# Giving the last split quarter of each gate and up tile its own buffers, and filling them one step later

## The chip, the cores and the metric

The kernel runs on one core of a Trainium2 chip. A core has a matrix engine (PE in the profile, with its weight loads shown apart as PEld), a vector engine (DVE), a scalar engine (ACT), a third elementwise engine (POOL) and a queue (SP) that issues most of the transfers from main memory. All of them run side by side and wait for each other through semaphores. The metric is the time of one execution in microseconds; less is better.

## The reference

One step of a decoder trunk over 520 tokens (512 new ones and 8 single continuations), width 1024, all in 32-bit floats: a half-step feed-forward block, a mixer, a second half-step feed-forward block and a last normalization. The change touches only the two feed-forward blocks:

```
def _swiglu(x, wg, wu, wd):
    return (jax.nn.silu(x @ wg) * (x @ wu)) @ wd
h = h + 0.5 * _swiglu(_rms_norm(h, ffn1_norm), ffn1_w_gate, ffn1_w_up, ffn1_w_down)
...
h = h + 0.5 * _swiglu(_rms_norm(h, ffn2_norm), ffn2_w_gate, ffn2_w_up, ffn2_w_down)
```

The gate and up matrices are 1024 by 2816, the down matrix 2816 by 1024. The 2816 columns are 22 tiles of 128, counted f = 0 to 21.

## The kernel before, in words

**Numbers in two parts.** A 32-bit product is computed as three faster ones. A weight tile is split into a rounded part (`whi`, a cast on ACT, L106) and the remainder (`wlo`, a subtraction on DVE, L107); `mm3` (L116 to L118) then issues high by high, high by low and low by high. Such a pair of buffers comes from the function `split`, whose buffers are 1024 columns wide and belong to a named ring: `whi`/`wlo` with three buffers each, `shi`/`slo` with two each.

**A step.** For each f from 2 (first block) or 1 (second block) on, the tokens are taken in two halves and gate and up together in seven products instead of eight, a scheme that multiplies sums of weight tiles with sums of token tiles. `load(f)` fetches the raw gate and up tiles (two transfers of 512 KB, L250 and L251, into one of two buffers of the ring `raw`), splits the gate tile (`d1`, traced as whi_fa), forms sums of quarters (`s1` at L257, `s2` at L258 and L259), splits these (`e1`, `e2`, traced as shi_fc and shi_fd) and splits the last quarter of the up tile, 512 columns (`d2`, traced as whi_fb). `product(f, p)` is one of the seven: twelve matmuls (four pieces of depth times three). Product 4 is the only one that uses `d2`. ACT copies intermediate sums out of the accumulators (`ac`, L285), `gates` and `close` make the activated tile `g` (L291 to L301).

**The order in which `step` asks for them.** product(f, 1), which calls `load(f)`; then product(f-1, 4) and close(f-1); then the products 5, 6, 3, 7, 2 of f. So product 4 of a tile comes one step after its other six.

**Chunks.** After tiles 0 to 7, 8 to 15 and 16 to 21 of g, the down product runs over what is there: eight output tiles d, each with a weight unit of up to 1024 columns that `load_unit` loads into half of a `raw` buffer and splits into the ring `whi`/`wlo` (48 matmuls a unit in the first two chunks; traced as whi_1d and whi_2d, dn). Before it, product(hi+1, 1), product(hi, 4) and close(hi) are asked for, so that at this edge one tile of the next chunk is loaded already. In the last chunk of the second block (`down_by_half`) units 0 and 1 are split into `whi`/`wlo`, 2 and 3 into `shi`/`slo`, and 4 to 7 into buffers of their own that become free when product(21, 4) is done.

**What sets the order on an engine.** The program is written down once in the order above; then a planner with a modelled timeline lays out, for each engine and for the transfer queue, the instructions that can run, earlier-written ones first, so that products of the next tile may fill a time in which an earlier-written matmul isn't ready. On the chip every engine follows its list strictly: an instruction that waits holds up all behind it. A buffer of a ring is given to its next user when the last reader of its previous content is done, and a transfer waits in the queue until its buffer is free.

**In the second block** sixteen small state updates go along with the steps: two transfers in on SP (`br`, `hs`, L796 and L798), eight scalings on ACT (L813), and an adding and a storing transfer from POOL (L814, L815).

The change's lines are `split`, the end of `load`, and the head of `product`.

Of the kernel before, what the change touches and what calls it, by code (L numbers as in the profile page):

```python
# [10 lines left out]
F32R = mybir.dt.float32r  # L11
# [5 lines left out]
P = 128  # L17
# [44 lines left out]
def tile_trunk_step(ctx: ExitStack, tc: tile.TileContext, ins: dict, outs: dict):  # L62
# [7 lines left out]
    wp = ctx.enter_context(tc.tile_pool(name="wp", bufs=3, side="right"))  # L70
# [19 lines left out]
    def raw_pair(name):  # L90
        return wp.tile([P, 2, 1024], F32, tag="raw", bufs=2, name=f"raw_{name}")
# [6 lines left out]
            half.extend([t[:, 1], t[:, 0]])  # L98
        return half.pop()

    def split(src, n, name, hp, nb, tags):
        hi, lo = (hp.tile([P, 1024], F32R, tag=t, bufs=nb, name=f"{t}_{name}")[:, :n] for t in tags)
        h, l = hi, lo
        if len(src.shape) == 3:
            h, l = (t.rearrange("p (j c) -> p j c", j=src.shape[1]) for t in (hi, lo))
        nc.scalar.copy(h, src)  # L106
        nc.vector.tensor_tensor(out=l, in0=src, in1=h.bitcast(F32), op=ALU.subtract)  # L107
        return hi, lo

    def load_unit(src, n, name):  # L110
        raw = raw_tile(name)[:, :n]
        nc.sync.dma_start(out=raw, in_=src)
        return split(raw, n, name, wp, 3, ("whi", "wlo"))

    def mm3(ps, whi, wlo, xhi, xlo, start, stop, **kw):
        nc.tensor.matmul(ps, whi, xhi, start=start, stop=False, **kw)  # L116
        nc.tensor.matmul(ps, whi, xlo, start=False, stop=False, **kw)  # L117
        nc.tensor.matmul(ps, wlo, xhi, start=False, stop=stop, **kw)  # L118

    def ws(w, k, m=P):  # L120
        return w[:, k * m : (k + 1) * m]
# [73 lines left out]
    class Ffn:  # L195
# [50 lines left out]
        def load(self, f):  # L246
            i, wx, src = self.i, self.wx, ins[f"w{self.i}gu"]
            n = f"{i}_{f}"
            raw = raw_pair(n)
            nc.sync.dma_start(out=raw[:, 0], in_=src[2 * f])  # L250
            nc.sync.dma_start(out=raw[:, 1], in_=src[2 * f + 1])  # L251
            d1 = split(raw[:, 0], 1024, f"{n}a", wp, 3, ("whi", "wlo"))
            s1 = wx.tile([P, 2, 512], F32, tag="sw", bufs=2, name=f"s1_{n}")
            s2 = wx.tile([P, 2, 512], F32, tag="sw", bufs=2, name=f"s2_{n}")
            up0 = raw[:, 1, :512].unsqueeze(1).to_broadcast([P, 2, 512])
            diag = bass.AP(up0.tensor, up0.offset - 1024, [up0.ap[0], (1536, 2), up0.ap[2]])
            nc.vector.tensor_tensor(out=s1, in0=diag, in1=up0, op=ALU.add)  # L257
            nc.vector.tensor_tensor(out=s2[:, 0], in0=s1[:, 1], in1=raw[:, 0, :512], op=ALU.add)  # L258
            nc.vector.tensor_tensor(out=s2[:, 1], in0=s2[:, 0], in1=raw[:, 0, 512:], op=ALU.add)  # L259
            e1 = split(s1.rearrange("p q c -> p (q c)"), 1024, f"{n}c", wx, 2, ("shi", "slo"))  # L260
            e2 = split(s2.rearrange("p q c -> p (q c)"), 1024, f"{n}d", wx, 2, ("shi", "slo"))
            d2 = split(raw[:, 1, 512:], 512, f"{n}b", wp, 3, ("whi", "wlo"))
            self.w[f] = {1: (d1, 0), 2: (d1, 4), 7: (e1, 0), 5: (e1, 4), 6: (e2, 0), 3: (e2, 4), 4: (d2, 0)}

        def product(self, f, p):
            js = range(KD // 2)
            if f not in self.A:
                with tc.issue_after(self.behind[f]) if f in self.behind else nullcontext():
                    self.load(f)
                n = f"{self.i}_{f}"  # L270
                self.A[f] = ps[0].tile([P, 512], F32, tag="A", bufs=2, name=f"A{n}")
                self.BE[f] = ps[0].tile([P, 2, 512], F32, tag="BE", bufs=2, name=f"BE{n}")
                self.ac[f] = [self.wx.tile([P, 2, HB], F32, tag="ac", bufs=3, name=f"ac{n}_{q}") for q in range(2)]
            slot, dst, opens = {1: (0, 0, True), 2: (1, 1, True), 5: (3, 2, True), 6: (5, 0, False),
                                3: (2, 2, False), 7: (4, 0, False), 4: (6, 0, False)}[p]
            out = self.A[f] if dst == 0 else self.BE[f][:, dst - 1]
            (whi, wlo), k0 = self.w[f][p]
            xth, xtl = self.nx[:2]
            for j in js:
                mm3(out[:, :HB], ws(whi, k0 + j), ws(wlo, k0 + j), xth[:, j, slot], xtl[:, j, slot], opens and j == 0,  # L280
                    j == KD // 2 - 1, skip_group_check=True)
            a, c = self.ac[f]
            keep = {1: a[:, 0], 6: a[:, 1], 7: c[:, 0], 5: c[:, 1]}.get(p)
            if keep is not None:
                nc.scalar.copy(keep, out[:, :HB])  # L285
            if p == 7:
                nc.vector.tensor_tensor(out=c[:, 0], in0=c[:, 0], in1=c[:, 1], op=ALU.add)
# [797 lines left out]
```

## Time and profile before

| what | value |
|---|---|
| runs, median (lowest to highest) | 1020.13 us (1017.38 to 1020.46), 3 runs |
| profiled execution, its own time | 1019.81 us |
| profiled execution, span | 1018.0 us |
| granted PE clock over the span | 0.992 |
| first block, steps and downs | about 26 to 360 us of the span |
| mixer | about 350 to 640 us |
| second block | about 640 to 1000 us |

The profile has a page with the busy share of each engine, and views that answer for a stretch of time or for a tile: the instructions in order of time (start, duration, engine, line, operation, names, shape, count, and in brackets the idle time before it with what ended it), the waits summed over the span (total, times, longest), and the busy time of each engine in given windows (duration of the window, then busy time and count for PE, PEld, DVE, ACT and POOL, the granted clock, the share of the transfer engines and GB/s).

### The profile page before, as it was taken

Reading aid. Unit: us, or ns where it says so; the run is one execution under the profiler, and the core shown is the slowest. Engines: PE = TensorE matmul, PEld = TensorE weight load, DVE = VectorE, ACT = ScalarE, POOL = GpSimd, SP = SyncE. Lnnn points to the kernel's source line nnn. Section 1 sums busy time; section 2 is a strip of 40 time slices with the busy share of each in tenths; the row PEclk is TensorE's granted clock in tenths of the full one; section 3 lists DMA queues with packets and bytes.
Section 4 is the critical chain, followed back from the end, with each engine's and each line's share of the span. In section 5 each row is a group of like instructions: output and inputs, shape, how many; then the busy total and the mean of one; then the engine's idle time right before and its main releaser. Section 6 shows DMA issues by size and latency. Waiting matters only on the chain.

```text
span 1018.0 us, 19402 instructions
## 1 busy us (share of the span) xinstructions
PE 979.7 (96%) x7850; PEld 955.5 (94%) x7850; DVE 790.3 (78%) x1344; ACT 539.9 (53%) x941; POOL 82.8 (8%) x141
## 2 busy tenths in 40 slices
PE   7999999999999999999999989999999999999994
PEld 6999999999999999999899989899999999999993
DVE  7899556995569688688989987999745898447865
ACT  7566323664146455685854235668623787226542
POOL 0000000000000000157211000001100111001000
PEclk9999999999999999999999999999999999999997
DMA  5333222332223232353244321335623556334303
GB/s 175 125 124 120 89 83 87 122 98 101 93 83 104 86 109 106 113 188 116 90 144 149 116 83 53 124 111 163 189 97 115 159 181 187 126 97 135 104 32 84
DMA packets 49193, 118.65 MB, mean 117 GB/s; under 512 B 6664, under 2 KB 17864, under 8 KB 49104
## 3 DMA queue, kind: packets, MB, share of 16 engines
q1 hardware_dynamic: 45520, 109.03, 32.5%
q0 software_dynamic: 3584, 8.39, 3.5%
q8 instruction: 61, 1.00, 0.4%
q14 instruction: 28, 0.23, 0.1%
HBM read 105.86 MB, written 7.34 MB: 111 GB/s over the span
## 4 chain that ended last, share of the span: by engine, by line
PE 85%; DVE 5%; ACT 5%; issue 2%; DMA 2%; POOL 0%; SPq 0%; DVEq 0%; ACTq 0%
PE dn L116 7%; PE dn L118 7%; PE dn L117 7%; PE A L116 7%; PE A L117 6%; PE A L118 6%; PE BE L116 5%; PE BE L118 5%; PE BE L117 5%; PE P L229 4%; PE wo L116 2%; PE wo L118 2%; PE wo L117 2%; PE inz L116 2%; PE inz L118 2%
## 5 line engine op out<-in xcount | busy, mean ns | idle before, releaser
L357 DVE SCALAR_TENSOR_TENSOR td<-dn,r_f 128x520 f32<-128x520 f32 x40 | 27.8, 698 | 112.8 <-PE dn L118 112.8
L116 PE MATMUL dn<-g,whi_1d 128*128 128x260 f32 x352 | 99.5, 283 | 1.8 <-ACT whi_1d L106 1.6
L117 PE MATMUL dn<-g,whi_1d 128*128 128x260 f32 x352 | 99.5, 283 | 0.0
L118 PE MATMUL dn<-g,wlo_1d 128*128 128x260 f32 x352 | 99.1, 282 | 0.0
L116 PE MATMUL dn<-g,whi_2d 128*128 128x260 f32 x256 | 72.5, 283 | 1.6 <-ACT whi_2d L106 1.6
L117 PE MATMUL dn<-g,whi_2d 128*128 128x260 f32 x256 | 72.3, 282 | 0.0
L118 PE MATMUL dn<-g,wlo_2d 128*128 128x260 f32 x256 | 72.2, 283 | 0.0
L116 PEld LDWEIGHTS dn<-g,whi_1d 128*128 128x128 f32 x352 | 66.2, 188 | 2.4 <-ACT whi_1d L106 2.0
L117 PEld LDWEIGHTS dn<-g,whi_1d 128*128 128x128 f32 x352 | 66.3, 188 | 0.0
L118 PEld LDWEIGHTS dn<-g,wlo_1d 128*128 128x128 f32 x352 | 66.1, 188 | 0.0
L285 ACT COPY ac<-A 128x260 f32<-128x260 f32 x123 | 45.7, 373 | 32.2 <-PE A L118 31.3
L106 ACT CAST whi_1d<-raw_1d 128x1024 fp32r<-128x1024 f32 (+1 forms) x24 | 23.4, 979 | 70.8 <-PE dn L117 62.4
L257 DVE TENSOR_TENSOR s<-raw 128x1024 f32<-128x1024 f32 x41 | 49.9, 1218 | 3.8 <-DMA raw<-in_w2gu 3.7
L106 ACT CAST whi_2d<-raw_2d 128x1024 fp32r<-128x1024 f32 (+1 forms) x18 | 18.5, 1027 | 63.4 <-PE dn L117 59.3
L229 PE MATMUL P<-xg_f,raw 128*128 128x260 f32 x192 | 46.4, 401 | 5.9 <-DMA raw<-in_w1gu 5.9
L116 PEld LDWEIGHTS dn<-g,whi_2d 128*128 128x128 f32 x256 | 48.3, 189 | 2.0 <-ACT whi_2d L106 2.0
L229 PEld LDWEIGHTS P<-xg_f,raw 128*128 128x128 f32 x192 | 37.8, 200 | 12.2 <-ACT sq_f L154 5.9
L117 PEld LDWEIGHTS dn<-g,whi_2d 128*128 128x128 f32 x256 | 48.2, 188 | 0.0
L118 PEld LDWEIGHTS dn<-g,wlo_2d 128*128 128x128 f32 x256 | 48.0, 188 | 0.0
L117 PE MATMUL wo<-catg,whi_wo 128*128 128x260 f32 x128 | 36.4, 285 | 1.3 <-DVE catg L942 1.3
L116 PE MATMUL wo<-catg,whi_wo 128*128 128x260 f32 x128 | 37.3, 293 | 0.3 <-DVE h L911 0.3
L814 POOL DMA_DIRECT2D hs<-so x16 | 13.9, 868 | 282.6 <-ACT hs L813 144.3
(1338 smaller groups left out, 3973.3 us busy)
## 6 DMA issues: line engine op xcount, KB each, us to landing
raw<-in_w2gu SPq DMA_DIRECT2D x44, 512.0 KB, 4.5
raw<-in_w1gu SPq DMA_DIRECT2D x42, 512.0 KB, 4.4
raw_1d<-in_w1d SPq DMA_DIRECT2D x16, 512.0 KB, 4.4
raw_2d<-in_w2d SPq DMA_DIRECT2D x16, 512.0 KB, 4.6
raw_wo<-in_w_out SPq DMA_DIRECT2D x12, 512.0 KB, 4.9
ab<-scr_acs SPq DMA_DIRECT2D x8, 512.0 KB, 4.6
h<-in_state_ssm SPq DMA_DIRECT2D x16, 256.0 KB, 4.1
raw_inz<-in_w_in SPq DMA_DIRECT2D x8, 512.0 KB, 4.0
```

The source lines that it names most:

```text
L106: nc.scalar.copy(h, src)
L116: nc.tensor.matmul(ps, whi, xhi, start=start, stop=False, **kw)
L117: nc.tensor.matmul(ps, whi, xlo, start=False, stop=False, **kw)
L118: nc.tensor.matmul(ps, wlo, xhi, start=False, stop=stop, **kw)
L229: nc.tensor.matmul(self.banks[f, u][b][:, :HB], ws(self.raw[f][:, u], j + 4 * q), xg[:, slot[q]], start=j == q == 0, stop=j == 3 and q == ...
L257: nc.vector.tensor_tensor(out=s1, in0=diag, in1=up0, op=ALU.add)
L285: nc.scalar.copy(keep, out[:, :HB])
L357: nc.vector.scalar_tensor_tensor(out=t, in0=banks[d][:, :, :HB], scalar=-0.5, in1=self.nx[3].rearrange("p (b t) -> p b t", b=2), op0=ALU.mult,
L814: nc.gpsimd.dma_start(out=hs, in_=o, accum_op=ALU.add)
```

## The change

`d2` leaves the three-buffer ring `whi`/`wlo` of 1024 columns. It gets a ring of its own, `uhi`/`ulo`, with one buffer each of 512 columns, in the pool that also holds the `g` tiles. `split` takes the width of its buffers as an argument for this. The split isn't made in `load(f)` any more: `load` leaves the raw tile in the table, and the first product of f other than product 1 makes it. In the written order that is product(f, 5), or product(21, 2) for the last tile, after product(f-1, 4) and close(f-1). As the ring has one buffer, the split of f waits for product(f-1, 4) to finish; and the raw buffer of f is held until that split is done. No arithmetic changes.

```
-    def split(src, n, name, hp, nb, tags):
-        hi, lo = (hp.tile([P, 1024], F32R, tag=t, bufs=nb, name=f"{t}_{name}")[:, :n] for t in tags)
+    def split(src, n, name, hp, nb, tags, cols=1024):
+        hi, lo = (hp.tile([P, cols], F32R, tag=t, bufs=nb, name=f"{t}_{name}")[:, :n] for t in tags)
...
-            d2 = split(raw[:, 1, 512:], 512, f"{n}b", wp, 3, ("whi", "wlo"))
-            self.w[f] = {1: (d1, 0), 2: (d1, 4), 7: (e1, 0), 5: (e1, 4), 6: (e2, 0), 3: (e2, 4), 4: (d2, 0)}
+            self.w[f] = {1: (d1, 0), 2: (d1, 4), 7: (e1, 0), 5: (e1, 4), 6: (e2, 0), 3: (e2, 4), 4: raw}
 
         def product(self, f, p):
...
+            if p != 1 and not isinstance(self.w[f][4], tuple):
+                d2 = split(self.w[f][4][:, 1, 512:], 512, f"{self.i}_{f}b", self.gp, 1, ("uhi", "ulo"), 512)
+                self.w[f][4] = d2, 0
```

## The prediction

> **What bounds the kernel now.** I read the page first, then the busy time by windows, then the waits of PE, then the engines in order of time at a chunk's edge, in an ordinary step and near the end.
>
> ```profile
> span 1018.0 us, 19402 instructions
> PE 979.7 (96%) x7850; PEld 955.5 (94%) x7850; DVE 790.3 (78%) x1344; ACT 539.9 (53%) x941; POOL 82.8 (8%) x141
> ```
>
> PE is busy 96% of the span, so all that any edit of buffers can win is in the 38.3 us in which it isn't. Where these are, windows show (duration, then PE, PEld, DVE, ACT, POOL, clock, transfers):
>
> ```profile
> 40.00:110.00 70.00, 69.91 (x581) 69.70 (x580) 64.87 (x89) 43.22 (x69) 0.00 (x0) 1.00 0.34 117
> 110.00:140.00 30.00, 29.00 (x240) 28.58 (x240) 12.06 (x16) 7.17 (x9) 0.00 (x0) 1.00 0.28 100
> 140.00:185.00 45.00, 45.00 (x378) 45.00 (x377) 33.01 (x45) 17.59 (x26) 0.00 (x0) 1.00 0.28 94
> 860.00:890.00 30.00, 28.88 (x236) 28.25 (x235) 15.02 (x20) 9.27 (x13) 0.57 (x1) 1.00 0.47 164
> ```
>
> The steps (40 to 110) and the rest of the chunk keep PE full; about 1 us is lost at each of the four edges between chunks (110 and 860 are the first and the last of them). The waits of PE name what ends these stops:
>
> ```profile
> PE A L116 <- ACT ac L285: 6.7, 8, 2.0
> PE dn L116 <- ACT whi_2d L106: 1.6, 2, 0.8
> PE dn L116 <- ACT whi_1d L106: 1.6, 2, 0.8
> PE A L118 <- DVE slo_8d L107: 0.8, 1, 0.8
> PE A L118 <- DVE slo_15d L107: 0.5, 1, 0.5
> ```
>
> The second and third rows are the four edges: a down matmul waits for the cast of its weight unit. The last two are steps of the second block that waited for a late split.
>
> **The change at the edges.** The first edge in order of time, ACT and then PE:
>
> ```profile
> 105.82 0.62 ACT L106 CAST whi_9b<-raw 128x512 fp32r<-128x512 f32 x1 [0.39 <-PE BE L117]
> 110.50 1.05 ACT L106 CAST whi_1d<-raw_1d 128x1024 fp32r<-128x1024 f32 x1 [0.77 <-PE A L117]
> 119.62 1.05 ACT L106 CAST whi_1d<-raw_1d 128x1024 fp32r<-128x1024 f32 x1 [5.00 <-PE dn L117]
> 121.07 1.04 ACT L106 CAST whi_1d<-raw_1d 128x1024 fp32r<-128x1024 f32 x1 [0.39 <-PE A L117]
> 121.11 0.28 PE L117 MATMUL dn<-g,whi_1d 128*128 128x260 f32 x1
> 122.17 0.39 PE L116 MATMUL dn<-g,whi_1d 128*128 128x260 f32 x1 [0.77 <-ACT whi_1d L106]
> ```
>
> Of three `whi` buffers, tile 9 holds two (its gate tile and, since 105.82, its last quarter). One is left, so the first unit is cast at 110.50, when product(8, 4) lets go, and the second only at 119.62, when the first unit's matmuls are over (ACT idled 5.00 us for it). PE stops from 121.11 to 122.17. The change takes the last quarters of 8 and 9 out of the ring: when unit 0 is split, another buffer is free for unit 1, some 9 us before PE wants it. A step (below) issues 87 matmuls in 10.09 us, 0.12 each, so a stop costs 122.17 - 121.11 - 0.12 = 0.94 us, and four 3.8 us. Next in line are the raw units: they need a `raw` buffer that is now held longer (below, about 5 us), against a wait of 9 us between the casts of units 0 and 1; I take no loss there. The small `ac` waits at the same edges (part of the 6.7) I leave as they are.
>
> No instruction is added or removed; cast and subtraction keep their 512 columns. So all else is when they run, and whom they hold up. The extra buffers replace nothing else; that they move later tiles in memory has no row, and the neighbours (the `g` ring, the state tiles) are filled long before or after: 0, between -0.5 and +0.5 by the size of one such wait (slo_15d).
>
> **The change in an ordinary step.** Tiles 5 to 8 of the first block:
>
> ```profile
> 77.54:87.63 10.09, 10.09 (x87) 10.09 (x86) 9.37 (x15) 6.33 (x11) 0.00 (x0) 1.00 0.30 104
> 75.54 0.62 ACT L106 CAST whi_6b<-raw 128x512 fp32r<-128x512 f32 x1 [0.38 <-PE BE L117]
> 76.94 0.68 DVE L107 TENSOR_TENSOR wlo_6b<-raw,whi_6b 128x512 fp32r<-128x512 f32 x1
> 77.65 0.33 SPq L250 DMA_DIRECT2D raw<-in_w1gu  x1
> 81.11 0.28 PE L118 MATMUL A<-xth_f,wlo_5b 128*128 128x260 f32 x1
> 87.63 1.22 DVE L257 TENSOR_TENSOR s<-raw 128x1024 f32<-128x1024 f32 x1
> 94.29 1.05 ACT L106 CAST shi_8c<-s 128x1024 fp32r<-128x1024 f32 x1 [0.70 <-PE BE L117]
> raw<-in_w1gu SPq DMA_DIRECT2D x42, 512.0 KB, 4.4
> ```
>
> Now the split of 6 ends at 77.62 and at 77.65 SP sends for the tiles of 8 into the buffer so freed; DVE reads them at 87.63. After the change the split of 6 waits for product(5, 4), over at 81.11 + 0.28 = 81.39; with cast and subtraction it ends at 82.69 at the earliest, 5.1 us later, and the load of 8 moves with it. The pair lands about 0.4 (two issues) + 4.4 after, at 87.5: just ahead of 87.63, with nothing to spare if ACT or DVE is on another instruction (up to 1.22 each) when the split becomes ready. What covers a slip: the sums aren't cast before 94.29, so DVE can do other work of the step first, and it has 10.09 - 9.37 = 0.72 us of idle a step. What has no cover: DVE keeps its list, and a sum placed too early in it holds up the gates and the next splits behind it. Behind the load on SP stand only other loads in this block. The split itself is needed by product(6, 4) ten us later: no wait. On ACT the cast waits for PE but is listed where it's planned to be ready. I take 0 for the first block; its bounds are 0 below (the windows are full, so there is nothing to win) and, if DVE idles 1.22 a step, 1.22 - 0.72 = 0.5 for each of some 16 steps, 8 us.
>
> The second block is closer to the edge. Its step in which the load comes late today (PE, ACT, DVE, SP, then the transfer from the chain of waits, and what followed):
>
> ```profile
> 712.13 0.28 PE L118 MATMUL A<-xth_f,wlo_6b 128*128 128x260 f32 x1
> 710.58 0.39 ACT L813 ACTIVATE so<-br,sxdt 128x128 f32<-128x128 f32 x1
> 712.63 0.39 ACT L813 ACTIVATE hs<-hs,sdec 128x128 f32<-128x128 f32 x1
> 708.70 0.68 DVE L107 TENSOR_TENSOR wlo_7b<-raw,whi_7b 128x512 fp32r<-128x512 f32 x1
> 714.04 0.33 SPq L798 DMA_DIRECT2D hs<-in_state_ssm  x1
> 714.47 0.37 SPq L250 DMA_DIRECT2D raw<-in_w2gu  x1
> 714.89 5.70 DMA raw<-in_w2gu
> 720.71 1.23 DVE L257 TENSOR_TENSOR s<-raw 128x1024 f32<-128x1024 f32 x1 [1.98 <-DMA raw<-in_w2gu]
> 723.73 0.39 PE L118 MATMUL A<-xth_f,slo_8d 128*128 128x260 f32 x1 [0.76 <-DVE slo_8d L107]
> ```
>
> The buffer of 7 was free at 709.38, but on SP the `hs` load stood ahead until 714.04, so the pair was sent for at 714.47 and landed 6.1 us later; DVE idled 1.98 and PE 0.76 (1.03 with the slower restart, 0.39 against 0.12). By the change the split of 7 would wait for 712.41 (product(6, 4)), then for the block of eight scalings to 713.02, then 0.62 + 0.68: 714.32. So this step gets no worse, but every step of this block becomes about as late as this one. In the plan the lateness is known, so the sum goes later in DVE's list; what counts is how much later than planned the transfers land beside the state transfers. I take +0.5 us over the block, half of what one such late step costs; bounds are -1.3 (both waits of today gone, 0.76 + 0.50) and 16 steps at 1.03, 16.5 us.
>
> **The change at the end of the second block.** There the last raw buffer feeds units 2 and 3:
>
> ```profile
> 958.97 0.28 PE L118 MATMUL A<-xth_f,wlo_20b 128*128 128x260 f32 x1
> 953.59 0.68 DVE L107 TENSOR_TENSOR wlo_21b<-raw,whi_21b 128x512 fp32r<-128x512 f32 x1
> 963.71 0.84 ACT L106 CAST shi_2d<-raw_2d 128x768 fp32r<-128x768 f32 x1 [2.37 <-PE BE L117]
> 967.27 0.28 PE L116 MATMUL dh<-g,shi_2d 128*128 128x260 f32 x1
> raw_2d<-in_w2d SPq DMA_DIRECT2D x8, 384.0 KB, 3.7
> ```
>
> The split of 21 ends at 954.27 now; after, at 959.25 + 0.62 + 0.68 = 960.55. The two units land 0.4 + 3.7 later, about 964.7, and unit 2 is cast from 964.3 or so instead of 963.71; PE uses it at 967.27. Units 6 and 7 come after them in the same buffer. I take +0.8 (cast and subtraction no longer hidden by some 0.6 us, and as little again for the following pair); bounds 0 and 2.4, a whole load moved past its cover (6.3 us later against 963.71 - 954.27 - 4.1 = 5.3 of slack, with one cast and one subtraction behind).
>
> **The sum.** 1019.81 (profiled execution; 1.8 outside its span) - 3.8 + 0 + 0.5 + 0.8 = 1017.3 us, 0.25% below it. The median of the runs shown, 1020.13, is 0.3 above that execution. A difference of 0.3%, 3.1 us, is about what a measurement of this kernel can tell from no change; the forecast lies just inside.
>
> **The rivals.**
> First, late loads: the sum on DVE (L257) is listed before its tiles land, and in the second block step after step repeats 720.71. For it speaks that loads there take 6.1 us against 4.8 in the first and that DVE has only 0.72 us of slack; against it that the list is drawn up with the later load in it and that 94.29 leaves room. It decides when a pair lands more than 0.72 us after its place in DVE's list; at half to all of 1.03 in 16 steps it gives 8 to 16 us against the 3.8 won: 1024 to 1032, middle 1027, slower. The Trainium skill, "DMA: Bandwidth & Descriptors", section Bandwidth, lists 6.15 us for one transfer of 1 MB. An estimate from it lets the tiles of 8 land at 82.69 + 6.15 = 88.84, 1.2 us behind 87.63, and would put the first block into this rival too (1.2 - 0.72 = 0.5 a step, 8 us more); the second block's row (6.1) agrees with that page, the first block's (4.8) doesn't.
> Second, nothing happens at the edges: units 0 and 1 come late in turn because their raw buffer is released 5 us later, so the stop stays with another releaser. Against it: 119.62 waited for PE, not for a transfer. It gives 1019 to 1021.
> Third, a luckier order: the eight `ac` waits (6.7 us, two of them near 2.0, both behind scalings on ACT) and the two late splits (1.3) also shrink, since ACT may cast gate tiles earlier. Half of the 8.0 more: 1013. Nothing in the rows forces it.
>
> **How the numbers follow.** Forecast 0.44 (its own range 1015 to 1020), late loads 0.36 (0.06 of it with the first block), no effect 0.08, luckier order 0.12. The forecast's case lies about half beyond 0.3%: faster 0.21 + 0.12 = 0.33, same 0.21 + 0.08 = 0.29, slower 0.36 + 0.02 = 0.38. The range leaves out the better half of the third rival and the worse third of the first: 1012 to 1029.
>
> **What the profile after would show.** At the edges: two casts of units before the first down matmul, and no PE wait for whi_1d or whi_2d. In the steps: cast of uhi right after product(f-1, 4), and SP's issue 5 us later than now in the first block, 0 to 5 in the second. If the first rival holds, DVE's waits for raw grow from two to many and PE waits for slo. At the end: PE waiting for shi_2d or a later unit. The prediction is wrong if 40 to 110 no longer fills PE, or if the edges still stop.

## The result, and the profile after

The changed kernel takes 1035.31 us (median of 5 runs, 1034.26 to 1037.51), the kernel before 1020.46 us beside it (5 runs, 1017.38 to 1023.11). The ratio is 1.0166, 95% interval 1.0146 to 1.0186: 1.7% slower, clear of the scatter of the runs, and outside the range of the prediction.

The page of the profile after has PE busy for about as long as before, in a longer span:

```profile
span 1033.5 us, 19348 instructions
PE 983.0 (95%) x7850; PEld 957.1 (93%) x7850; DVE 792.8 (77%) x1344; ACT 534.6 (52%) x941; POOL 82.6 (8%) x141
```

Where the 15.5 us of span are, the ends of products show. The last matmuls of product (2, 4) and of product (21, 4) in the second block, first before, then after:

```profile
671.81 0.28 PE L118 MATMUL A<-xth_f,wlo_2b 128*128 128x260 f32 x1
968.84 0.28 PE L118 MATMUL A<-xth_f,wlo_21b 128*128 128x260 f32 x1
```

```profile
671.81 0.28 PE L118 MATMUL A<-xth_f,ulo_2b 128*128 128x260 f32 x1
987.06 0.28 PE L118 MATMUL A<-xth_f,ulo_21b 128*128 128x260 f32 x1
```

At the end of product (2, 4) of the second block the two kernels are level to the hundredth. From there to product (21, 4) it takes 297.0 us before and 315.2 after: 18.2 more, of which 2.7 come back behind it (48.9 us to the end of the span before, 46.2 after). This stretch, "the second block" in what follows, is the measure for all experiments. The same stretch of the first block is 289.2 before and 288.1 after.

Busy time in windows shows the same (duration, then PE, PEld, DVE, ACT, POOL, clock, share of the transfer engines, GB/s). A window in the second block and this whole stretch, before:

```profile
690.00:735.00 45.00, 43.86 (x361) 43.23 (x361) 40.77 (x58) 35.62 (x76) 5.71 (x8) 1.00 0.64 193
672.10:969.12 297.02, 289.57 (x2374) 287.22 (x2374) 215.52 (x293) 167.48 (x333) 23.02 (x32) 0.99 0.45 139
```

and after, with the two windows of the first block that the prediction shows:

```profile
40.00:110.00 70.00, 69.27 (x572) 68.65 (x571) 63.88 (x87) 42.22 (x69) 0.00 (x0) 1.00 0.32 109
110.00:140.00 30.00, 29.54 (x246) 29.54 (x247) 15.09 (x20) 6.91 (x10) 0.00 (x0) 1.00 0.36 120
690.00:735.00 45.00, 36.85 (x291) 35.15 (x289) 33.35 (x46) 29.43 (x67) 4.29 (x6) 1.00 0.46 136
672.10:987.34 315.24, 295.66 (x2385) 291.05 (x2384) 216.82 (x294) 166.50 (x334) 23.07 (x32) 0.99 0.43 134
```

From 690 to 735 PE issues 291 matmuls where it issued 361, at full clock: it waits. No other engine is fuller there than before. Over the whole stretch PE is idle for 19.6 us where it was for 7.5, 12.1 of the 18.2; it is also busy 6.1 us longer, for eleven more matmuls. Part of that is clock: the trace after has two pieces of 3.4 us at half the granted clock in this stretch, the one before has one. The waits of PE after (total, times, longest):

```profile
PE A L116 <- ACT ac L287: 12.2, 12, 2.1
PE A L116 <- ACT shi_13d L106: 2.3, 1, 2.3
PE A L116 <- ACT shi_7d L106: 2.3, 1, 2.3
PE dn L116 <- ACT whi_2d L106: 1.6, 1, 1.6
```

PE waits for ACT. What ACT waits for, the instructions of all engines in order of time show, in steps 5 to 9 of the second block after:

```profile
689.48 1.05 ACT L106 CAST whi_6a<-raw 128x1024 fp32r<-128x1024 f32 x1 [3.06 <-DMA raw<-in_w2gu]
692.19 0.39 ACT L815 ACTIVATE so<-br,sxdt 128x128 f32<-128x128 f32 x1
694.24 0.39 ACT L815 ACTIVATE hs<-hs,sdec 128x128 f32<-128x128 f32 x1
695.05 0.62 ACT L106 CAST uhi_5b<-raw 128x512 fp32r<-128x512 f32 x1
695.71 0.69 DVE L107 TENSOR_TENSOR ulo_5b<-raw,uhi_5b 128x512 fp32r<-128x512 f32 x1
696.43 0.33 SPq L250 DMA_DIRECT2D raw<-in_w2gu  x1
702.12 1.05 ACT L106 CAST whi_7a<-raw 128x1024 fp32r<-128x1024 f32 x1 [2.12 <-DMA raw<-in_w2gu]
...
718.34 6.30 SPq L800 DMA_DIRECT2D hs<-in_state_ssm  x2
721.43 0.68 DVE L107 TENSOR_TENSOR ulo_7b<-raw,uhi_7b 128x512 fp32r<-128x512 f32 x1
724.73 0.38 SPq L250 DMA_DIRECT2D raw<-in_w2gu  x1
728.34 1.04 ACT L106 CAST whi_9a<-raw 128x1024 fp32r<-128x1024 f32 x1 [4.59 <-DMA raw<-in_w2gu]
730.24 0.64 ACT L287 COPY ac<-A 128x260 f32<-128x260 f32 x2
730.66 0.39 PE L116 MATMUL A<-xth_f,uhi_7b 128*128 128x260 f32 x1 [2.15 <-ACT ac L287]
```

It is a circle. The load of tile 7 goes out (696.43) when the last quarter of tile 5 is split (695.05, 695.71). The cast of gate tile 7 waits for it (702.12), and ACT, which keeps its list, does nothing else meanwhile. On ACT the cast of a gate tile stands ahead of the last quarter one tile back, as 689.48 (tile 6) stands ahead of 695.05 (tile 5); between them are the eight scalings (692.19 to 694.63) and the copies `ac` that PE waits for. So load, gate cast, scalings, last quarter and next load follow each other. The second group shows the same with SP in it: the split of 7 is over at 722.11, but the load of 9 stands behind an `hs` load until 724.73.

### The profile page after: what moved, and what is told of

The parts are those of the page before. It is cut to its first block, busy times and chain, and to the rows that moved or that the text cites. A ratio compares the mean times of both kernels' runs of the same rounds, so it can differ in the third digit from the quotient of the medians.

```text
span 1033.5 us, 19348 instructions
## 1 busy us (share of the span) xinstructions
PE 983.0 (95%) x7850; PEld 957.1 (93%) x7850; DVE 792.8 (77%) x1344; ACT 534.6 (52%) x941; POOL 82.6 (8%) x141
## 5 line engine op out<-in xcount | busy, mean ns | idle before, releaser
L106 ACT CAST whi_2d<-raw_2d 128x1024 fp32r<-128x1024 f32 (+1 forms) x18 | 18.5, 1028 | 57.8 <-PE dn L117 51.2
L293 DVE TENSOR_TENSOR tg<-BE,ac 128x520 f32<-128x520 f32 x41 | 28.5, 696 | 13.6 <-PE BE L118 11.9
L117 PE MATMUL wo<-catg,whi_wo 128*128 128x260 f32 x128 | 36.4, 285 | 1.3 <-DVE catg L944 1.2
```

Source lines behind the costliest of these rows:

```text
L293: nc.vector.tensor_tensor(out=tg, in0=self.BE[f][:, :, :HB], in1=self.ac[f][0], op=ALU.add)
```

## The experiments

In what follows, the home is the new ring `uhi`/`ulo` with one buffer, and a late quarter is a last quarter that is split one step later. The texts on what was expected call PE TensorE, ACT ScalarE, DVE VectorE and POOL GpSimd. All experiments use the same measure beside the total: the time between the ends of product (2, 4) and product (21, 4) in each block. Where a ratio is given, it is to the kernel before on the same chip (1017.9 to 1018.7 us for e1 to e18), with its 95% interval.

| run | us | ratio (interval) | first block | second block |
|---|---|---|---|---|
| before | 1020.46 | 1 | 289.2 | 297.0 |
| after | 1035.31 | 1.0166 (1.0146 to 1.0186) | 288.1 | 315.2 |
| e1 change in first block only | 1020.04 | 1.0015 (0.9996 to 1.0035) | 287.9 | 299.1 |
| e2 change in second block only | 1049.81 | 1.0308 (1.0282 to 1.0334) | 289.1 | 327.3 |
| e3 after, gate cast held back | 1036.21 | 1.0176 (1.0150 to 1.0203) | 288.4 | 315.8 |
| e4 after, state loads on POOL's queue | 1032.0 | 1.0139 (1.0105 to 1.0172) | 288.2 | 307.6 |
| e5 late filling, old ring | 1008.92 | 0.9911 (0.9893 to 0.9928) | 285.4 | 290.2 |
| e6 own home, filled at once | 1033.97 | 1.0165 (1.0141 to 1.0189) | 288.3 | 311.0 |
| e7 before, no state work | 1022.40 | 1.0040 (1.0026 to 1.0055) | 288.8 | 288.7 |
| e8 after, no state work | 1021.23 | 1.0033 (1.0021 to 1.0044) | 286.9 | 288.7 |
| e9 after, no scalings | 1013.02 | 0.9941 (0.9917 to 0.9965) | 288.2 | 289.8 |
| e10 after, no state transfers | 1042.79 | 1.0234 (1.0211 to 1.0256) | 287.2 | 306.6 |
| e11 e2 with e4's queue | 1038.07 | 1.0184 (1.0158 to 1.0210) | 289.2 | 313.2 |
| e12 e5 with e4's queue | 1005.48 | 0.9868 (0.9844 to 0.9892) | 285.4 | 287.8 |
| e13 after, scalings behind the cast | 1029.24 | 1.0105 (1.0086 to 1.0124) | 288.3 | 305.4 |
| e14 after, scalings ahead of the cast | 1042.47 | 1.0224 (1.0201 to 1.0247) | 288.5 | 314.5 |
| e15 before, no scalings | 1009.98 | 0.9911 (0.9896 to 0.9926) | 289.2 | 288.6 |
| e16 before, no state transfers | 1030.91 | 1.0119 (1.0102 to 1.0136) | 288.8 | 297.2 |
| e17 after, scalings on POOL | 1029.74 | 1.0103 (1.0065 to 1.0141) | 288.7 | 303.2 |
| e18 e5, scalings on POOL | 1032.62 | 1.0131 (1.0091 to 1.0171) | 285.4 | 314.0 |

The lengths of the blocks come from one profiled execution of each kernel. e1's second block, which e1 leaves as it was, is 2.1 us longer than that of the kernel before, so differences of that size are not read. The last column and the whole time don't always move together. Against the changed kernel the second block is shorter by 7.6 us in e4, 9.8 in e13, 12.0 in e17 and 0.7 in e14; the whole time is shorter by 3.3, 6.1 and 5.6, and in e14 longer by 7.2. Part of this lies between the two measured stretches: from the first block's product (21, 4) to the second block's product (2, 4) it takes 335.6 us in e14 and 335.7 in e17, 332.5 after, and in both 6.8 us of it, from 653 us on, run at half the granted clock.

### Which block: e1 and e2

In `load` the last quarter stays where it was in the other block (shown for e1; e2 has 2 in place of 1):

```
-            self.w[f] = {1: (d1, 0), 2: (d1, 4), 7: (e1, 0), 5: (e1, 4), 6: (e2, 0), 3: (e2, 4), 4: raw}
+            d2 = raw
+            if i != 1:
+                d2 = split(raw[:, 1, 512:], 512, f"{n}b", wp, 3, ("whi", "wlo")), 0
+            self.w[f] = {1: (d1, 0), 2: (d1, 4), 7: (e1, 0), 5: (e1, 4), 6: (e2, 0), 3: (e2, 4), 4: d2}
```

> The change in the first feed-forward block alone; the second splits at once into the old ring. Theory: the loss comes from the second block alone, where the cast of the next gate tile stands on ACT ahead of its transfer (ACT waited 3.06, 2.12 and 4.59 us for raw between 689 and 729). Then this kernel is within 1 us of the kernel before, since the first block of the changed kernel ended product(21, 4) at 339.6 us against 340.2. Rival (both blocks lose, or the place of the buffers in memory does): some 1 to 8 us slower.

> The change in the second block alone. Theory: the whole loss, 14 to 17 us slower than before, with ACT again waiting for raw ahead of whi casts. Rival (the loss needs both blocks): clearly less than 14.

The first block alone changes nothing that can be told apart from no change; the loss is in the second. But there the change costs 31 us alone, and 16 with both blocks, so e2's size was not expected. The lists of ACT, PE and DVE differ little between the two kernels; on SP the state load `hs` stands ahead of a weight load in one more step of e2 (see e11). PE's granted clock over the second block is also lower in e2, 0.97 against 0.99.

### Whose wait: e3 and e4

e3 holds back the gate tile's cast until the tile g two steps back is cast, so that ACT has it late in its list; e4 moves the two state loads to POOL's queue.

```
-            d1 = split(raw[:, 0], 1024, f"{n}a", wp, 3, ("whi", "wlo"))
+            with tc.issue_after(self.closed[f - 2]) if f - 2 in self.closed else nullcontext():
+                d1 = split(raw[:, 0], 1024, f"{n}a", wp, 3, ("whi", "wlo"))
...
-            nc.scalar.copy(g[:, 0], tg)
+            self.closed[f] = nc.scalar.copy(g[:, 0], tg).ins
```

```
-            tc.keep_in_program_order(nc.sync.dma_start(out=br, in_=rows_bc(b, 0, g)))
+            tc.keep_in_program_order(nc.gpsimd.dma_start(out=br, in_=rows_bc(b, 0, g)))
...
-            tc.keep_in_program_order(nc.sync.dma_start(out=hs, in_=ins["state_ssm"][:, b, 4 * g : 4 * g + 4]))
+            tc.keep_in_program_order(nc.gpsimd.dma_start(out=hs, in_=ins["state_ssm"][:, b, 4 * g : 4 * g + 4]))
```

> The changed kernel with one more order on ACT: the cast of gate tile f comes after the cast of g of tile f-2, which is about where the old ring put it. Buffers, the late fill and the later loads stay. Theory (the freed ring lets the planner list this cast early, and there it holds up the copies behind it): at least 8 of the 15.5 us come back, 1020 to 1028, and ACT's waits for raw ahead of whi are nearly gone. Rival (the later load itself is the loss, wherever the cast stands): 1032 to 1038, and the wait moves to DVE's sums or to the splits.

> The changed kernel with the two small state loads (br and hs) issued from the POOL queue instead of SP, so that the loads of gate and up tiles stand behind none of them. Theory (the load is late by two delays in a row, the held buffer and the hs load that waits on SP for the store before it): about half of the loss comes back, 1022 to 1030. Rival (the held buffer alone makes the load late): within 2 us of the changed kernel, 1033 to 1038.

In e3 ACT's waits for the raw gate tiles from tile 3 on are gone, and the time is the same. The wait only changed engines, as the waits of DVE in the second block of e3 show:

```profile
DVE s L258 <- DMA raw<-in_w2gu: 20.8, 10, 3.7
```

So it is not the place of the cast in ACT's list that makes the load late; the list only decides who stands still. e4 lies between its two ranges: it brings back 3.3 us of the whole time and 7.6 of the second block, so SP's queue has a part in it. The same edit without the home (e12 against e5, below) brings 3.4 and 2.4 us.

### Which half of the change: e5 and e6

e5 fills late, but from the old ring; e6 has the home of its own, filled in `load` as before.

```
-                d2 = split(self.w[f][4][:, 1, 512:], 512, f"{self.i}_{f}b", self.gp, 1, ("uhi", "ulo"), 512)
+                d2 = split(self.w[f][4][:, 1, 512:], 512, f"{self.i}_{f}b", wp, 3, ("whi", "wlo"))
```

```
-            self.w[f] = {1: (d1, 0), 2: (d1, 4), 7: (e1, 0), 5: (e1, 4), 6: (e2, 0), 3: (e2, 4), 4: raw}
+            d2 = split(raw[:, 1, 512:], 512, f"{n}b", self.gp, 1, ("uhi", "ulo"), 512)
+            self.w[f] = {1: (d1, 0), 2: (d1, 4), 7: (e1, 0), 5: (e1, 4), 6: (e2, 0), 3: (e2, 4), 4: (d2, 0)}
...
-            if p != 1 and not isinstance(self.w[f][4], tuple):
-                d2 = split(self.w[f][4][:, 1, 512:], 512, f"{self.i}_{f}b", self.gp, 1, ("uhi", "ulo"), 512)
-                self.w[f][4] = d2, 0
```

> Late filling alone, in both blocks: the split last quarter is again a tile of the old ring of three, but is still filled one step later. In that ring its buffer is the one that product (f-1,2) releases, so it does not wait for product (f-1,4). Theory home (the single buffer of the home, released only by product (f-1,4), holds the raw tile): loads of pair f+2 are issued as early as before, the cast of the next gate tile stays behind product (f-1,4), and the time is 1017 to 1024 us. Theory late filling (a split that is filled a step later holds the raw tile, wherever it goes): 1030 to 1038 us, ScalarE's waits for raw tiles in the second block over 12 us, as in the changed kernel.

> The home of its own alone, in both blocks: the split last quarter has the single small buffer, but is written in the load as before. Theory home: the split still waits for product (f-1,4), the raw tile is held as long as in the changed kernel, and the time is 1029 to 1040 us, with 12 to 25 us of ScalarE's waits for raw tiles in the second block. Theory late filling: 1016 to 1023 us.

The home alone costs as much as the whole change. Late filling alone is 0.9% faster than the kernel before, which neither theory had. Its gain includes what the prediction wanted from the home: the profile of e5 has no wait of PE for whi_1d or whi_2d any more. The first edge in e5, SP and ACT, and the window that lost 1.00 us of PE before:

```profile
97.26 28.77 SPq L112 DMA_DIRECT2D raw_1d<-in_w1d  x6
105.25 1.06 ACT L106 CAST whi_1d<-raw_1d 128x1024 fp32r<-128x1024 f32 x1 [0.39 <-PE BE L117]
112.11 1.06 ACT L106 CAST whi_1d<-raw_1d 128x1024 fp32r<-128x1024 f32 x1 [2.95 <-PE A L117]
151.21 0.62 ACT L106 CAST whi_9b<-raw 128x512 fp32r<-128x512 f32 x1 [4.69 <-PE dn L117]
110.00:140.00 30.00, 30.00 (x253) 30.00 (x252) 13.16 (x17) 6.16 (x7) 0.00 (x0) 1.00 0.28 95
```

The last quarter of tile 9 now takes its buffer behind all eight units (151.21), so units 0 and 1 are cast at 105.25 and 112.11 where they were at 110.50 and 119.62, and PE doesn't stop. The steps between the edges are unharmed, since in the ring of three the late quarter gets the buffer that product (f-1, 2) gives back and doesn't wait for product (f-1, 4).

### What in the second block: e7 to e10, e15, e16

e7 and e8 are before and after without any state work (in e7 to e10, e15 and e16 the new state isn't computed):

```
-        def load(b, g):
...
+        nc.gpsimd.dma_start(out=outs["nss"], in_=ins["state_ssm"])
+        while True:
+            yield
```

e9 and e15 are after and before with the transfers and no scalings, e10 and e16 with the scalings and no transfers:

```
-            o = wx.tile([P, 4, P], F32, tag="so", bufs=2, name=f"so{b}{g}")
-            for q in range(4):
...
+        o = wx.tile([P, 4, P], F32, tag="so", bufs=2, name="so0")
+        nc.gpsimd.memset(o, 0.0)
```

```
-                for t, u, s in ((o, br, sxdt), (hs, hs[:, q], sdec)):
+                for t, s in ((o, sxdt), (hs, sdec)):
                     tc.keep_in_program_order(
-                        nc.scalar.activation(out=t[:, q], in_=u, func=AF.Copy, scale=s[:, j, b : b + 1]))
-            nc.gpsimd.dma_start(out=hs, in_=o, accum_op=ALU.add)
-            nc.gpsimd.dma_start(out=outs["nss"][:, b, 4 * g : 4 * g + 4], in_=hs)
+                        nc.scalar.activation(out=t[:, q], in_=ident, func=AF.Copy, scale=s[:, j, b : b + 1]))
...
```

> The kernel before without the work on the sample states in the second block: the loads of state and row, the 128 scalings on ScalarE and the two stores of each step are left out, and the new state is one copy of the old one in DRAM, so the new state is not computed. It is the control of the next run. Both theories: 1008 to 1019 us (ScalarE is not the bound there, so little changes).

> The changed kernel without the same state work (the new state is a copy, not computed). Theory crowding (the held raw tile costs time in the second block and none in the first because there the loads stand behind the state loads on SP, share the DMA engines with them, and the casts share ScalarE with eight scalings a step): 0 to 4 us above the control. Theory holding alone (the later load is too late in the second block whatever else runs): 10 to 16 us above the control, as with the state work.

> The changed kernel with the state loads, adds and stores of the second block, but without their 128 scalings on ScalarE: a tile of zeros is added, so the new state is not computed (it is a copy of the old one). Theory ScalarE (the loss needs the eight scalings a step, which take 8 x 0.39 us on ScalarE between the cast of the late tile and the copies that TensorE waits for): the loss goes, 1006 to 1016 us. Theory transfers (the loss comes from the state transfers, on SP's queue and on the DMA engines): it stays, 1026 to 1036 us.

> The changed kernel with the 128 scalings, but of a resident tile: none of the state loads, adds and stores of the second block is issued, and the new state is one copy of the old one in DRAM at the start, as in the two runs without state work, so the new state is not computed. The control is the run of the kernel before without state work, 1022.4 us, which pays the same copy at the start. Theory ScalarE: the loss is back, 1030 to 1036 us. Theory transfers: 1019 to 1025 us. If the loss needs both (transfers that make the scalings late, and scalings that make the transfers late), both this run and the one without scalings are near their controls.

> Control: the kernel before with the state loads, adds and stores and without the 128 scalings (a tile of zeros is added, the new state is not computed). Both theories: 1006 to 1018 us, so that the changed kernel without scalings (1013.0 us) is within some 5 us of it.

> Control: the kernel before with the 128 scalings of a resident tile and without the state transfers (the new state is one copy of the old at the start, not computed). Both theories: 1018 to 1028 us, so that the changed kernel with the same edit (1042.8 us) stands 15 us or more above it.

The totals of e7, e8, e10 and e16 carry some 13 us at the start, where their copy of the whole state runs beside the first weight load (the waits of PE in e7):

```profile
PE P L229 <- DMA raw<-in_w1gu: 18.5, 1, 18.5
```

That is why e7 and e16 came out above what was expected of controls; e16 also has the scalings' own price, and so has e10, which lies above its range. e10 stands 11.9 us above its control e16, where 15 or more were expected. The lengths of the second block are free of the start:

| second block, us | before | after | difference |
|---|---|---|---|
| no state work (e7, e8) | 288.7 | 288.7 | 0.0 |
| transfers alone (e15, e9) | 288.6 | 289.8 | 1.2 |
| scalings alone (e16, e10) | 297.2 | 306.6 | 9.4 |
| both | 297.0 | 315.2 | 18.2 |

Without state work the change is free in the second block, as in the first. Transfers alone add next to nothing; scalings alone bring half of the loss, and the transfers the other half when scalings are there. By the whole times the four differences are -1.2, 3.0, 11.9 and 14.9 us, so how the loss divides between scalings and transfers is known only roughly. The theory of crowding holds, and within it ScalarE's part comes first. The steady step without state work (ACT in e8) shows the circle closing in time:

```profile
703.81 0.62 ACT L106 CAST uhi_5b<-raw 128x512 fp32r<-128x512 f32 x1 [0.90 <-PE A L117]
708.78 1.05 ACT L106 CAST whi_7a<-raw 128x1024 fp32r<-128x1024 f32 x1 [0.86 <-DMA raw<-in_w2gu]
713.91 0.62 ACT L106 CAST uhi_6b<-raw 128x512 fp32r<-128x512 f32 x1 [0.90 <-PE A L117]
```

From one late quarter to the next are 10.10 us (703.81 to 713.91), one step of PE. The gate cast already waits for its load, and the late quarter then waits 0.90 us for product (f-1, 4): that is all the slack there is. Eight scalings take 2.44 us in a row (692.19 to 694.63 above). In the changed kernel the same distance is 11.51 us from tile 5 (695.05, above) to tile 6:

```profile
706.56 0.62 ACT L106 CAST uhi_6b<-raw 128x512 fp32r<-128x512 f32 x1
```

### The place of the scalings: e13 and e14

`step` asks for the state work after product (f, 6) in e13 and after product (f, 5) in e14, instead of at its head:

```
-            if self.states is not None and f > 2:
-                next(self.states, None)
...
             for p in (2, 5, 6, 3, 7) if f == KF - 1 else (5, 6, 3, 7, 2):
                 self.product(f, p)
+                if p == 6 and self.states is not None and f > 2:
+                    next(self.states, None)
```

> The changed kernel with the state work of each step asked for two products later, so that ScalarE has the same eight scalings behind the late quarter's cast instead of ahead of it; nothing is left out. Theory loop (the raw tile is released by the late quarter's cast, its load feeds the cast of the gate tile two steps on, and that stands on ScalarE ahead of the next late quarter's cast: a loop that has to close within a TensorE step of 10.1 us, and the scalings stand in it): behind the cast they fall into the wait for the load, the loop closes in 10.1 to 10.8 us, and the time is 1008 to 1020 us. Theory sum (the scalings cost by their time on ScalarE wherever they stand): 1028 to 1036 us as in the changed kernel.

> The same with the state work asked for one product later only: in ScalarE's list the scalings then stand right ahead of the late quarter's cast in every step, so inside the loop in all of them. Theory loop: 1030 to 1046 us, with over 12 us from one late quarter's cast to the next. Theory sum: 1028 to 1036 us. A time under 1022 us would be against both.

The same work at two places differs by 13 us of the whole time and 9.1 of the second block, so the place counts. e14's whole time lies in the range of the theory of the loop and 6 us above that of the sum. But its second block is no longer than that of the changed kernel (314.5 and 315.2 us), so its 7 us more don't speak for the loop; its late quarters are 11.4 to 13.1 us apart from tile 4 to tile 8, where the loop expected over 12. And e13 gives back 6 us, within the range of the sum, and not the 15 to 27 of the loop. So the circle through the load is not all of it, and neither theory holds alone. In e13 ACT has, in one step:

```profile
695.22 0.62 ACT L106 CAST uhi_5b<-raw 128x512 fp32r<-128x512 f32 x1 [0.90 <-PE A L117]
697.56 0.41 ACT L815 ACTIVATE so<-br,sxdt 128x128 f32<-128x128 f32 x1
700.44 1.05 ACT L106 CAST shi_6c<-s 128x1024 fp32r<-128x1024 f32 x1
706.09 0.62 ACT L106 CAST uhi_6b<-raw 128x512 fp32r<-128x512 f32 x1 [0.90 <-PE A L117]
```

The step is 10.87 us (695.22 to 706.09) with no wait for a load in it. The scalings now stand ahead of the cast of a sum (700.44), which PE needs in the same step.

### Queues, and the scalings on POOL: e11, e12, e17, e18

e11 and e12 are e2 and e5 with e4's edit. e17 and e18 are after and e5 with the scalings on POOL:

```
-                        nc.scalar.activation(out=t[:, q], in_=u, func=AF.Copy, scale=s[:, j, b : b + 1]))
+                        nc.gpsimd.tensor_scalar(out=t[:, q], in0=u, scalar1=s[:, j, b : b + 1], scalar2=None, op0=ALU.mult))
```

> The change in the second block alone (1049.8 us), with the state loads on GpSimd's queue. In that kernel SP's list has the state load one place ahead of the weight load of some steps, where the changed kernel has it behind. If that is why it is 15 us slower than the change in both blocks, it comes to 1030 to 1037 us here; if not, it stays at 1045 us or more.

> Late filling from the old ring (1008.9 us) with the state loads on GpSimd's queue. As no stop in that kernel's second block stood with a state load, it is within 3 us of it: 1005 to 1011 us. Theory transfers would see 3 us or more back here too: 1004 to 1006 us.

> The changed kernel with the 128 scalings on GpSimd in place of ScalarE; nothing is left out. If ScalarE's list is the whole cause: 1010 to 1018 us, as without the scalings (1013.0 us). If what matters is that the state work has to be done within a step, wherever (GpSimd takes an estimated 0.8 us for each of eight, by the nearest row of the trace of before, 0.79 us for a copy of 128x120, against 0.39 on ScalarE, and its adds and stores stand behind them): the stores land later, the state loads hold up SP's queue longer, and the time stays at 1026 us or more.

> Late filling from the old ring (1008.9 us) with the 128 scalings on GpSimd. In the kernel before, leaving the scalings out brought 8.7 us (1018.7 to 1010.0). If GpSimd's work is free beside VectorE's: 1000 to 1006 us. If it slows VectorE or the state transfers: 1008 us or more.

e11 takes 12 of the 31 us away, a us short of what was expected. e2 is 14.5 us above the change in both blocks; with the state loads of both on POOL's queue (e11 and e4) 6.1 are left. So somewhat more than half of the difference goes through SP, where the two kernels' lists differ in two places of the second block. e12 is the fastest kernel of the study, 1.3% below the kernel before; it lies in both of its ranges and doesn't decide between them. e17 gives back 6 us, not the 17 to 25 expected if ACT's list were the whole cause; e18 loses 24 us against e5. A group of POOL in e18 (busy us, mean ns of one, idle before), the wait of DVE in its second block, and one scaling and one such wait in order of time:

```profile
L815 POOL TENSOR_SCALAR so<-br,sxdt 128x128 f32<-128x128 f32 x64 | 70.8, 1106 | 157.2 <-PE A L118 88.0 <-DMA br<-scr_bc 68.7
DVE s L257 <- DMA raw<-in_w2gu: 25.1, 8, 6.1
685.41 0.59 POOL L815 TENSOR_SCALAR so<-br,sxdt 128x128 f32<-128x128 f32 x1
690.45 1.23 DVE L257 TENSOR_TENSOR s<-raw 128x1024 f32<-128x1024 f32 x1 [6.07 <-DMA raw<-in_w2gu]
```

A scaling takes 1.0 to 1.1 us on POOL in the mean, against 0.39 on ACT; while DVE stands still, as at 685.41, it takes 0.59. Eight of them and the two transfers behind them fill most of a step, the state loads on SP wait for their buffers, and the weight loads stand behind them. In e18, where the home of one buffer is gone, the second block is 23.8 us longer than in e5: for 14.8 of these PE is idle, and for 9.1 it is busy longer with the same 2375 matmuls, at a granted clock of 0.96 over the block.

### What is shown, and what isn't

Shown: the loss is in the second block (e1, e2), it comes from the home of one buffer and not from late filling (e5, e6), and it needs the state work beside it, the scalings above all (e7 to e10, e15, e16). Read from the traces and not separated by a run: how much of it goes through the circle of load and cast, how much through ACT's casts of sums that stand behind the scalings (e13), and how much through SP (by e4 3.3 us of the whole time or 7.6 of the second block; 12 between e2 and e11). The home brings three things at once: one buffer in place of three, gate casts that can be listed earlier, and other places in memory for later tiles. e3 speaks against the second, e8 (no loss without state work) against a cost of the third by itself. That it is the single buffer is argued from the circle; a home of two buffers wasn't tried.

## Why the prediction was wrong

**The edges (-3.8).** Nothing came of it; the second rival describes what happened, and one of the prediction's own signs of being wrong, edges that still stop, was there. The first edge after, SP, ACT and PE:

```profile
103.66 0.80 SPq L112 DMA_DIRECT2D raw_1d<-in_w1d  x2
107.46 1.05 ACT L106 CAST whi_1d<-raw_1d 128x1024 fp32r<-128x1024 f32 x1 [1.22 <-DMA raw_1d<-in_w1d]
109.37 1.04 ACT L106 CAST whi_1d<-raw_1d 128x1024 fp32r<-128x1024 f32 x1
110.46 0.39 PE L116 MATMUL dn<-g,whi_1d 128*128 128x260 f32 x1 [0.78 <-ACT whi_1d L106]
```

In the kernel before, SP sent for these units from here on:

```profile
97.83 10.90 SPq L112 DMA_DIRECT2D raw_1d<-in_w1d  x4
```

The second unit is cast early, as forecast (109.37 in place of 119.62). But the raw buffer comes 5.8 us later (103.66), so both units are late for PE, which now reaches the edge's down product before either is fully split: it stops 0.78 where it stopped 0.77 before. The cast that ends this stop is the second one (109.37 + 1.04 = 110.41). Before, too, it was the one behind the cast that the prediction names: the one at 121.07, over at 122.11, and not the one at 119.62, over at 120.67. The step that failed is "against a wait of 9 us between the casts of units 0 and 1; I take no loss there": those 9 us covered unit 1. Unit 0, cast at 110.50 and used soon after, had no such cover, and the same sentence moved its load by 5 us. The gain itself is real and was put on the wrong half of the change: e5, which moves only the filling, ends all four stops. It takes 3.8 us off the first block and 6.8 off the second, more than the edges alone; that the first of these equals the forecast for four edges is chance, as two of them lie there.

**The first block's steps (0).** Right. The load goes out where the prediction put it, and the circle closes within PE's step. The late quarters of tiles 6 and 7, and between them the load and the sum of tile 8 (ACT, SP, DVE, ACT):

```profile
81.97 0.62 ACT L106 CAST uhi_6b<-raw 128x512 fp32r<-128x512 f32 x1 [0.90 <-PE A L117]
83.47 0.33 SPq L250 DMA_DIRECT2D raw<-in_w1gu  x1
89.91 1.22 DVE L257 TENSOR_TENSOR s<-raw 128x1024 f32<-128x1024 f32 x1
92.07 0.62 ACT L106 CAST uhi_7b<-raw 128x512 fp32r<-128x512 f32 x1 [0.90 <-PE A L117]
```

They are 10.10 us apart. Of the 70 us from 40 to 110 PE is busy 69.27, 69.91 before; a wait of 0.41 at 41.10 and the beginning of the edge's stop make the difference, and from 52 to 100 PE is busy throughout. DVE's sums wait for no tile (0.1 us idle ahead of 41 of them in the groups of the profile after):

```profile
L257 DVE TENSOR_TENSOR s<-raw 128x1024 f32<-128x1024 f32 x41 | 50.0, 1218 | 0.1
```

The estimate of 8 us more from the Trainium skill ("DMA: Bandwidth & Descriptors", section Bandwidth, 6.15 us for 1 MB) didn't come (288.1 us against 289.2): the second transfer of this pair was sent at 83.84 and landed 4.3 us later, 4.7 behind the issue of the first, where the prediction had 4.8 and the estimate 6.15. The sum stands 6.4 us behind that issue (83.47 to 89.91), so even the page's figure would have been covered.

**The second block's steps (+0.5).** Here the prediction failed: 18.2 us, above its bound of 16.5. "Every step of this block becomes about as late as this one" was right. What failed is the next step: "In the plan the lateness is known, so the sum goes later in DVE's list; what counts is how much later than planned the transfers land". The sum did go later and DVE didn't wait. But the raw tile has a second reader, the gate cast on ACT, and the change frees its ring of three, so it could be listed early; there the wait stands ahead of the copies that PE needs. And lateness adds up: 714.32 was worked out for the split of 7 from the products of before. After, the split was over at 722.11, because each late step moves product (f-1, 4), for which the next split waits. A price per step, taken from one late step that the next one recovers, can't show that. What the runs showed in place of +0.5 is a circle with 0.90 us of slack (e8) that 2.44 us of scalings a step and the state transfers overrun: 18.2 us over the block. e3 says that another list alone wouldn't have helped, and the table of e7 to e16 says what ended the slack.

**The end of the block (+0.8).** The sign was wrong: the stretch behind product (21, 4) is 2.7 us shorter after, though it has one new stop, right behind that product:

```profile
987.86 0.39 PE L116 MATMUL dh<-g,shi_2d 128*128 128x260 f32 x1 [0.52 <-DVE tg L300]
```

In the trace after, 45 of the 288 last down matmuls start ahead of the end of product (21, 4), 34 in the one before: eleven at 0.12 us are 1.3 of the 2.7. The granted clock over this stretch is 0.89 after and 0.87 before, which is some of the rest; it wasn't followed further.

**The rivals and the range.** Late loads were the right rival, at 0.36, with the wrong engine and too low a price: it comes on top of no gain at the edges, while its 1024 to 1032 kept the 3.8 us. 1019.81 + 18.2 - 2.7 = 1035.3 is the profiled execution's time. The range ended at 1029 because it left out the worse third of the first rival and took the two as alternatives; they share one cause, the raw buffer held longer, and came together. The third rival had it reversed: the `ac` waits went from 6.7 to 12.2 us.

## What to carry to other kernels

A home of its own with one buffer isn't a gift: its next user waits for the last reader of the content, and whatever that user's source occupies is held as long. Before pricing it, follow the circle from the held buffer through the load and its readers back to the release, and compare its length with the step; if they are nearly equal, work on the way can cost time in step after step, on an engine that is half idle too. Here the plain variant, the same ring filled later, had the gain and none of the loss.

## What the runs showed of the hardware that was not expected

- 128 scalings of 0.39 us on ACT, which is busy 53% of the span, lengthen the second block of the kernel before by 8.4 us (288.6 in e15, 297.0), while its 64 state transfers alone lengthen it by nothing (288.7 in e7 and 288.6 in e15).
- Multiplying 128x128 values by one scalar a row takes 1.0 to 1.1 us on POOL in the mean of e18, over twice as long as on ACT (0.39). The time goes with what DVE does meanwhile: the 33 of them that ran wholly beside an idle DVE took 0.59 to 0.61 us, the 58 that ran wholly beside a busy one 1.33 in the mean and up to 2.4.
- Within the second block the granted clock falls to half for pieces of 3.4 or 6.8 us: one in the kernel before, two after, four in e2 and in e18 and none in e5, e7, e8 and e15. In the one from 743.60 to 747.05 after, 17 matmuls take 3.45 us, 0.20 each in place of 0.12. What sets one off isn't shown.
- A copy of 4.19 MB within main memory, issued at the start, holds up the first weight load: PE's wait for it is 18.5 us long (e7), 12.6 more than in the kernel before.
